# Average pooling 2x2, stride 2: the output of four loads gathered in one shared ring and stored as 63.5 KB per partition

## Chip, cores, metric

One core of one Trainium2 chip. The metric is device time in microseconds (us), the median of several executions; all runs quoted are of the fast state (the single look at one kernel has no state). The granted clock is 1.000 throughout and plays no part: nothing runs on TensorE.

## The reference

```python
# x: (32, 128, 256, 256) float32, kernel_size 2, stride 2
for i in range(h_out):
    for j in range(w_out):
        window = x[:, :, 2*i : 2*i + 2, 2*j : 2*j + 2]
        output[:, :, i, j] = np.mean(window, axis=(2, 3))
# output: (32, 128, 128, 128) float32
```

1073.7 MB are read and 268.4 MB written, each byte once. A *unit* below is one output row per partition: two input rows (2 KB) in, 512 bytes out, for each of 128 partitions. There are 4096 units.

## The kernel before

```python
sbuf = ctx.enter_context(tc.tile_pool(name="sbuf", bufs=2))
# plan: 126 parts of 32 units, then parts of 16, 8, 8 and 8, 8, 8, 4, 2, 1, 1
for parts in plan:
    in_tile = sbuf.tile([P, 32, 512], f32, name="in_tile")        # 64 KB per partition, two of them
    for g in parts:
        nc.sync.dma_start(out=it, in_=xt)                         # load queue: 64 KB per partition
        nc.vector.tensor_add(out=it[:, :, 0:w], in0=it[:, :, 0:w], in1=it[:, :, w : 2 * w])
        col_sum = sbuf.tile([P, 32, 128], f32, name="col_sum", bufs=3)
        nc.vector.tensor_add(out=col_sum[:, :g], in0=it[:, :, 0:w:2], in1=it[:, :, 1:w:2])
        nc.scalar.mul(out=col_sum[:, :g], in_=col_sum[:, :g], mul=0.25)
        nc.scalar.dma_start(out=ot, in_=col_sum[:, :g])           # store queue: 16 KB per partition
# (cut: index arithmetic, the generic path, the launch)
```

An input buffer is free again after the second add. A load is one packet of 64 KB per partition, eight per DMA engine (16 engines, 128 partitions); a store is one packet of 16 KB per partition, eight per engine.

## Time and profile before

| | before |
|---|---|
| time | 3106.51 us (3106.36 to 3106.79, 4 runs) |
| VectorE / ScalarE / DMA engines busy | 54% / 15% / all of the span |
| bytes over the span | 432 GB/s |
| one steady period (32 units) | 24.17 us |

The prediction shows the lines for these. One more view, the list of DMA issues, whose last column is the median time from issue to landing:

```profile
out_dram<-col_sum ACTq DMA_DIRECT2D x126, 2048.0 KB, 31.6
...
in_tile<-in_x_dram SPq DMA_DIRECT2D x126, 35.1
```

A 2 MB store is worth 4.8 us at 434 GB/s, yet lands 31.6 us after issue. An estimate of why: it waits about 7 us (31.6 - 24.2) for the store before it, then its eight packets per engine take turns with eight load packets: 8 x (0.61 + 2.42) = 24.2 us.

### The profile page before, as it was taken

The page shows a single profiled execution, that of the slowest core. Times are in us where ns is not written, and L with a number is a line of the kernel's source. Part 1 is how long each engine was busy: PE and PEld are TensorE (multiplying, and loading weights), DVE is VectorE, ACT ScalarE, POOL GpSimd, SP SyncE. Part 2 cuts the span into 40 slices and gives each one's busy share as a digit, 9 for nine tenths or more (in the row PEclk, how much of TensorE's full clock was granted, in tenths as well). Part 3 has the DMA queues.
Part 4 walks back from the last instruction along what each step waited for, and adds up shares of the span by engine and source line. Part 5 has one row for each costly group of instructions (what it writes and reads, how often), then busy time and mean ns, then how long its engine had stood idle before and what let it go on. Part 6 is the DMA issues. An engine that isn't in the chain of part 4 may idle for free. (4 is left out here: it accounts for less than half of the span.)

```text
span 3104.8 us, 1126 instructions
## 1 busy us (share of the span) xinstructions
DVE 1681.4 (54%) x272; ACT 465.8 (15%) x137; POOL 0.2 (0%) x4
## 2 busy tenths in 40 slices
DVE  4555555555555555555555555555555555555556
ACT  1111111111111111111111111111111111111112
POOL 0000000000000000000000000000000000000000
DMA  9999999999999999999999999999999999999999
GB/s 418 436 439 425 436 439 425 436 438 429 433 439 430 431 439 434 427 439 435 426 438 436 427 437 436 428 436 437 427 436 437 428 436 437 429 435 437 432 431 396
DMA packets 39176, 1342.26 MB, mean 432 GB/s; under 512 B 4352, under 2 KB 4736, under 8 KB 5888
## 3 DMA queue, kind: packets, MB, share of 16 engines
q1 hardware_dynamic: 19584, 1073.75, 79.8%
q10 hardware_dynamic: 19584, 268.44, 20.2%
q14 instruction: 8, 0.07, 0.0%
HBM read 1073.74 MB, written 268.44 MB: 432 GB/s over the span
## 5 line engine op out<-in xcount | busy, mean ns | idle before, releaser
L87 DVE TENSOR_TENSOR in_tile<-in_tile 128x8192 f32<-128x8192 f32 (+4 forms) x136 | 1113.9, 8190 | 1406.7 <-DMA in_tile<-in_x_dram 1406.7
L108 ACT ACTIVATE col_sum<-col_sum 128x4096 f32<-128x4096 f32 (+4 forms) x136 | 464.5, 3415 | 2635.9 <-DVE col_sum L96 2635.9
L96 DVE TENSOR_TENSOR col_sum<-in_tile 128x4096 f32<-128x4096 f32 (+4 forms) x136 | 567.8, 4175 | 13.9 <-DMA out_dram<-col_sum 1.8
L108 ACT ACT_TABLE_LOAD x1 | 1.3, 1283 | 0.7 <-PEq L190 0.7
L190 POOL MEMSET const-bfloat16-1.0<- 128x1 bf16 x1 | 0.1, 102 | 0.0
L190 POOL MEMSET const-uint8-127<- 128x1 uint8 x1 | 0.1, 102 | 0.0
L190 POOL MEMSET const-float32-0.0<- 128x1 f32 x1 | 0.1, 99 | 0.2 <-issue 0.2
L190 POOL MEMSET const-float32-1.0<- 128x1 f32 x1 | 0.1, 99 | 0.0
## 6 DMA issues: line engine op xcount, KB each, us to landing
out_dram<-col_sum ACTq DMA_DIRECT2D x126, 2048.0 KB, 31.6
in_tile<-in_x_dram SPq DMA_DIRECT2D x5, 2048.0 KB, 27.5
in_tile<-in_x_dram SPq DMA_DIRECT2D x1, 4096.0 KB, 25.5
out_dram<-col_sum ACTq DMA_DIRECT2D x5, 512.0 KB, 12.0
in_tile<-in_x_dram SPq DMA_DIRECT2D x126, 35.1
out_dram<-col_sum ACTq DMA_DIRECT2D x1, 1024.0 KB, 12.7
in_tile<-in_x_dram SPq DMA_DIRECT2D x1, 1024.0 KB, 16.2
in_tile<-in_x_dram SPq DMA_DIRECT2D x1, 512.0 KB, 16.9
```

The source lines that it names most:

```text
L87: nc.vector.tensor_add(out=it[:, :, 0:w], in0=it[:, :, 0:w], in1=it[:, :, di * w : (di + 1) * w],)
L96: nc.vector.tensor_add(out=col_sum[:, :g], in0=it[:, :, 0:wu:s], in1=it[:, :, 1 : wu + 1 : s],)
L108: nc.scalar.mul(out=col_sum[:, :g], in_=col_sum[:, :g], mul=inv)
L190: nc = _bacc.Bacc("TRN2", target_bir_lowering=False, num_devices=1)
```

## The change

The intent: fewer, longer stores and a better end. Output of four loads (31 + 32 + 32 + 32 = 127 units) collects in one buffer and leaves as one store of 63.5 KB per partition. The buffer is a ring of 158 units: groups lie alternately at units 0 to 126 and 31 to 157, so that the first piece of a group goes to the 31 units which the store under way does not read. The last group's store is issued on the load queue, behind the last loads, so that it covers the last pieces' arithmetic.

```diff
-    sbuf = ctx.enter_context(tc.tile_pool(name="sbuf", bufs=2))
-            col_sum = sbuf.tile([P, G_MAIN, w_out], mybir.dt.float32, name="col_sum", bufs=3)
-            nc.scalar.dma_start(out=ot, in_=col_sum[:, :g])
+IN_UNITS = 32
+GROUP = 127
+FIRST = GROUP - 3 * IN_UNITS
+    in_pool = ctx.enter_context(tc.tile_pool(name="inp", bufs=2))
+    out_pool = ctx.enter_context(tc.tile_pool(name="outp", bufs=1))
+    res = out_pool.tile([P, GROUP + FIRST, w_out], f32, name="res")
+    def pool(it, dst):
+        nc.vector.tensor_add(out=it[:, :, 0:w], in0=it[:, :, 0:w], in1=it[:, :, w:])
+        nc.vector.tensor_add(out=dst, in0=it[:, :, 0:w:2], in1=it[:, :, 1:w:2])
+        nc.scalar.mul(out=dst, in_=dst, mul=0.25)
+    for k in range(groups):                                       # 32 groups
+        base = 0 if k % 2 == 0 else FIRST
+        # pieces: the 31 units outside the store under way first, then 3 x 32
+        for a, g in pieces:
+            t = load(xt[:, a : a + g], g)
+            pool(t[:, :g], res[:, base + a : base + a + g])
+        if k < groups - 1:
+            nc.scalar.dma_start(out=ot, in_=res[:, base : base + GROUP])
+        else:
+            last = (ot, res[:, base : base + GROUP])
+    # rest of 32 units: loads of 16, 8, 8; then
+        if rest == 0:
+            nc.sync.dma_start(out=last[0], in_=last[1])
 (cut: index arithmetic, the pooling and storing of the rest, the old plan)
```

More of the change, by code (lines that the diff above doesn't have):

```diff
@@ L27 @@
     R = n * c * h_out
-    if k == s and 2 <= k <= 4 and R > 0 and R % P == 0:
-        _nonoverlap_pool(ctx, tc, x, out, k, n, c, h, w, h_out, w_out)
+    units = R // P if R % P == 0 else 0
+    if k == 2 and s == 2 and h % 2 == 0 and w == 256 and units >= 1024:
+        _pool_2x2(ctx, tc, x, out, units)
     else:
         _generic_pool(ctx, tc, x, out, k, s, n, c, h, w, h_out, w_out)
-def _nonoverlap_pool(ctx, tc, x, out, k, n, c, h, w, h_out, w_out):
+IN_UNITS = 32
+GROUP = 127
+FIRST = GROUP - 3 * IN_UNITS
@@ L36, in _nonoverlap_pool, with _pool_2x2 @@
+def _pool_2x2(ctx, tc, x, out, units):
     nc = tc.nc
     P = nc.NUM_PARTITIONS
-    s = k
-    R = n * c * h_out
-    hv = h_out * s
-    xs = x if hv == h else x[:, :, 0:hv, :]
-    xv = xs.rearrange("n c (ho a) w -> (n c ho) (a w)", a=s)
-    ov = out.rearrange("n c ho wo -> (n c ho) wo")
-    assert xv.shape == (R, s * w) and ov.shape == (R, w_out)
-    wu = w_out * s
-    unit_bytes = s * w * 4
-    G_MAIN = max(1, min(R // P, (64 * 1024) // unit_bytes))
-    total_units = R // P
-    nmain, rem_units = divmod(total_units, G_MAIN)
@@ L54, in _nonoverlap_pool @@
-    plan: list[list[int]] = [[G_MAIN] for _ in range(nmain)]
-    if rem_units:
-        plan.append([rem_units])
-    if G_MAIN % 32 == 0 and nmain >= 4 and rem_units == 0:
-        u = G_MAIN // 32
-        tail = [
-            [16 * u, 8 * u, 8 * u],
-            [8 * u, 8 * u, 8 * u, 4 * u, 2 * u, u, u],
-        ]
-        assert all(sum(t) == G_MAIN for t in tail)
-        plan = plan[:-2] + tail
-    sbuf = ctx.enter_context(tc.tile_pool(name="sbuf", bufs=2))
-    inv = 1.0 / float(k * k)
@@ L71, in _nonoverlap_pool @@
-    r0 = 0
-    for parts in plan:
-        in_tile = sbuf.tile([P, G_MAIN, s * w], mybir.dt.float32, name="in_tile")
-        g0 = 0
-        for g in parts:
-            rows = P * g
-            xt = xv[r0 : r0 + rows].rearrange("(p g) f -> p g f", p=P)
-            ot = ov[r0 : r0 + rows].rearrange("(p g) f -> p g f", p=P)
-            r0 += rows
-            it = in_tile[:, g0 : g0 + g]
-            g0 += g
-            nc.sync.dma_start(out=it, in_=xt)
-            for di in range(1, k):
-                nc.vector.tensor_add(
-                    out=it[:, :, 0:w],
-                    in0=it[:, :, 0:w],
-                    in1=it[:, :, di * w : (di + 1) * w],
-                )
-            col_sum = sbuf.tile(
-                [P, G_MAIN, w_out], mybir.dt.float32, name="col_sum", bufs=3
-            )
-            nc.vector.tensor_add(
-                out=col_sum[:, :g],
-                in0=it[:, :, 0:wu:s],
-                in1=it[:, :, 1 : wu + 1 : s],
-            )
-            for dj in range(2, k):
-                nc.vector.tensor_add(
-                    out=col_sum[:, :g],
-                    in0=col_sum[:, :g],
-                    in1=it[:, :, dj : wu + dj : s],
-                )
-            nc.scalar.mul(out=col_sum[:, :g], in_=col_sum[:, :g], mul=inv)
-            nc.scalar.dma_start(out=ot, in_=col_sum[:, :g])
-        assert g0 <= G_MAIN
@@ L113, in _nonoverlap_pool, with load @@
-    assert r0 == R, (r0, R)
+    f32 = mybir.dt.float32
+    w = x.shape[3]
+    w_out = w // 2
+    xv = x.rearrange("n c (ho a) w -> (n c ho) (a w)", a=2)
+    ov = out.rearrange("n c ho wo -> (n c ho) wo")
+    in_pool = ctx.enter_context(tc.tile_pool(name="inp", bufs=2))
+    out_pool = ctx.enter_context(tc.tile_pool(name="outp", bufs=1))
+    res = out_pool.tile([P, GROUP + FIRST, w_out], f32, name="res")
+    def load(src, g):
+        t = in_pool.tile([P, IN_UNITS, 2 * w], f32, name="in_tile")
+        nc.sync.dma_start(out=t[:, :g], in_=src)
+        return t
@@ new lines, in pool @@
+    def pool(it, dst):
+        nc.vector.tensor_add(out=it[:, :, 0:w], in0=it[:, :, 0:w], in1=it[:, :, w:])
+        nc.vector.tensor_add(out=dst, in0=it[:, :, 0:w:2], in1=it[:, :, 1:w:2])
+        nc.scalar.mul(out=dst, in_=dst, mul=0.25)
+    groups, rest = divmod(units, GROUP)
+    if rest == 0:
+        groups, rest = groups - 1, GROUP
+    last = None
+    for k in range(groups):
+        r0 = k * GROUP * P
+        xt = xv[r0 : r0 + GROUP * P].rearrange("(p g) f -> p g f", p=P)
+        ot = ov[r0 : r0 + GROUP * P].rearrange("(p g) f -> p g f", p=P)
+        base = 0 if k % 2 == 0 else FIRST
+        spans = [(FIRST + i * IN_UNITS, IN_UNITS) for i in range(3)]
+        if base == 0:
+            pieces = [(0, FIRST)] + spans
+        else:
+            pieces = [(3 * IN_UNITS, FIRST)] + [(a - FIRST, g) for a, g in spans]
+        for a, g in pieces:
[3 more added lines that the diff above has]
+            nc.scalar.dma_start(out=ot, in_=res[:, base : base + GROUP])
+        else:
+            last = (ot, res[:, base : base + GROUP])
@@ new lines, in _pool_2x2 @@
+    r0 = groups * GROUP * P
+    while rest:
+        n = min(rest, IN_UNITS)
+        t = in_pool.tile([P, IN_UNITS, 2 * w], f32, name="in_tile")
+        tout = in_pool.tile([P, IN_UNITS, 2 * w], f32, name="in_tile")
+        to = tout[:].rearrange("p g f -> p (g f)").rearrange("p (g f) -> p g f", f=w_out)
+        cuts = [n // 2, n // 4, n - n // 2 - n // 4] if n >= 8 else [n]
+        a, parts = 0, []
+        for g in cuts:
+            xt = xv[r0 : r0 + g * P].rearrange("(p g) f -> p g f", p=P)
+            ot = ov[r0 : r0 + g * P].rearrange("(p g) f -> p g f", p=P)
+            nc.sync.dma_start(out=t[:, a : a + g], in_=xt)
+            parts.append((ot, a, g))
+            a += g
+            r0 += g * P
+        rest -= n
+        if rest == 0:
+            nc.sync.dma_start(out=last[0], in_=last[1])
+        for ot, a, g in parts:
+            pool(t[:, a : a + g], to[:, a : a + g])
+            nc.scalar.dma_start(out=ot, in_=to[:, a : a + g])
```

## The prediction

> **What bounds the kernel now.** I read the page first, its busy shares and its row of DMA slices.
>
> ```profile
> DVE 1681.4 (54%) x272; ACT 465.8 (15%) x137; POOL 0.2 (0%) x4
> ...
> DMA  9999999999999999999999999999999999999999
> ...
> q1 hardware_dynamic: 19584, 1073.75, 79.8%
> q10 hardware_dynamic: 19584, 268.44, 20.2%
> ```
>
> VectorE works 54% of the span and ScalarE 15%, while the DMA engines stand at 9 in all forty slices: the load queue takes 79.8% of their time and the store queue 20.2%, together all of it. The bytes are fixed by the task: 1073.75 MB in, 268.44 MB out, 1342.2 MB. Second, the waits, to see who starves:
>
> ```profile
> ACT col_sum L108 <- DVE col_sum L96: 2635.9, 136, 33.9
> DVE in_tile L87 <- DMA in_tile<-in_x_dram: 1406.7, 133, 22.7
> DVE col_sum L96 <- DMA out_dram<-col_sum: 1.8, 3, 0.9
> ```
>
> VectorE waits for loads in 133 of 136 pieces; a wait for a store to free an output buffer exists three times, 1.8 us in all, at the very end. Third, the timeline of one steady stretch:
>
> ```profile
> 1494.01 8.69 DVE L87 TENSOR_TENSOR in_tile<-in_tile 128x8192 f32<-128x8192 f32 x1 [10.97 <-DMA in_tile<-in_x_dram]
> 1502.79 4.42 DVE L96 TENSOR_TENSOR col_sum<-in_tile 128x4096 f32<-128x4096 f32 x1
> ...
> 1507.25 3.62 ACT L108 ACTIVATE col_sum<-col_sum 128x4096 f32<-128x4096 f32 x1 [20.56 <-DVE col_sum L96]
> 1510.89 0.34 ACTq L110 DMA_DIRECT2D out_dram<-col_sum  x1
> 1518.19 8.69 DVE L87 TENSOR_TENSOR in_tile<-in_tile 128x8192 f32<-128x8192 f32 x1 [10.97 <-DMA in_tile<-in_x_dram]
> ```
>
> One period is 1518.19 - 1494.01 = 24.18 us (others 24.16); VectorE needs 8.69 + 4.43 = 13.1 us of it. A period moves 8.39 MB in and 2.10 MB out, so 10.49 MB in 24.17 us = 434 GB/s. Fourth, the same by stretches, to find where the rate is not 434:
>
> ```profile
> 2500.00:3000.00 500.00, 267.44 (x41) 75.47 (x21) 0.00 (x0) 1.00 1.00 433
> ...
> 3050.00:3060.00 10.00, 8.57 (x3) 3.48 (x1) 0.00 (x0) 1.00 0.98 419
> 3060.00:3070.00 10.00, 7.97 (x4) 3.10 (x3) 0.00 (x0) 1.00 1.01 434
> 3070.00:3080.00 10.00, 4.36 (x3) 1.06 (x1) 0.00 (x0) 1.00 1.01 431
> 3080.00:3090.00 10.00, 6.20 (x4) 1.87 (x2) 0.00 (x0) 1.00 0.99 419
> 3090.00:3100.00 10.00, 7.23 (x8) 2.33 (x4) 0.00 (x0) 1.00 0.82 332
> 3100.00:3104.80 4.80, 0.58 (x2) 0.63 (x3) 0.00 (x0) 1.00 0.33 111
> ```
>
> The last two columns are DMA share and GB/s. Only the last 15 us fall off. Against 434, the missing bytes of these six stretches are worth 0.35 + 0 + 0.07 + 0.35 + 2.35 + 3.57 = 6.7 us. That, the start, and the last fraction of a per cent between 434 and the ceiling are all a change of this kind can win.
>
> **What the Trainium skill says.** (1) "DMA: Bandwidth & Descriptors", section "Where 436 GB/s comes from": 16 ports give 435.2 GB/s. The trace agrees: 434 in the steady part and, in the first stretch without a store, 8.39 MB between the first add at 22.70 and the next at 42.02, so 19.32 us or 434 too. Loads alone and loads mixed with stores run at the same rate. (2) Same page, "Why small descriptors are slow (HBM only)": a fixed overhead of about 3 cycles per packet. The trace has something of that size: at 27.2 GB/s per engine, one engine's 8 x 65,536 + 8 x 16,384 bytes of a period take 24.094 us; measured 24.17, so 0.076 us over 18 packets (8 data and one semaphore packet in each of two queues): 4.2 ns a packet. (3) Same page, "Queues, rings and completion order": an engine goes round-robin between its queues, a packet of typically 9 to 17 descriptors at a time. The single-packet records of this trace show the turns but finer: around 1506 to 1512 us 32 load packets of 64 KB and 32 store packets of 16 KB start in 6.05 us, two of each per engine (2.42 + 0.61 us a pair), so one descriptor each in turn. (4) "SBUF — State Buffer", section "SBUF size: 192, 224, or 256?": about 208 KiB per partition are usable. The change takes 2 x 64 + 158 x 0.5 = 207 KiB; it fits barely, and no run yet shows it.
>
> **The change, part by part.**
> *Arithmetic.* The same adds and multiply on the same elements, in pieces of 31 or 32 units. VectorE stays near 1681 us, off the path: worth 0.
> *Fewer packets.* Before: 136 loads and 136 stores, 9 packets per engine each, 272 x 9 = 2448. After: 4096 units are 32 groups of 127 and a rest of 32, so 32 x 4 + 3 = 131 loads and 32 + 3 = 35 stores, 166 x 9 = 1494. The 954 packets fewer, at 4.2 ns, give 4.0 us. (The packet records would say more: 611 ns for 16 KB and 2418 for 64 KB fit 9.7 ns plus 36.7 ns per 1000 bytes, and 954 times 9.7 ns would be 9 us. But the durations overlap: summed over an engine they give 3107 us where the data lasted 3102. I take the 4.2 from the period.)
> *Bytes.* 1342.2 MB at 435.2 GB/s: 3084.1 us, before and after.
> *Tail.* Before, loads shrink to 256 KB, each followed by add, add, multiply and a store, so the DMA runs dry for 6 to 7 us. After, the last group's 8.3 MB store is issued behind the last three loads. Counting from the landing of the last full piece: its adds and multiply end at +16.7 us, when the store is issued; the last loads (8.39 MB, 19.3 us) still have about 2.6 us to go, so there is no gap. VectorE does the rest, 4.43 + 2.29 and twice 2.29 + 1.23 us, from +13.1 to about +27; the last small store is issued by +28. The DMA still has the 19.2 us big store plus 4.8 us of small ones, and is busy to about +43. It never runs dry; what remains is the last completion and the engines' uneven finish, estimated at 2.8 us (loads alone land 22.70 - 19.32 - 1.7 = about 1.7 us after their bytes would be through).
> *Sum.* Before: 3084.1 + 2448 x 0.0042 = 10.3, start 1.7 (first data packet), three hiccups in the 24.17 us rhythm 2.6, leaves 3104.8 - 3098.7 = 6.1 for the tail, near the 6.7 above. After: 3084.1 + 6.3 + 1.7 + 2.6 + 2.8 = 3097.5 us of span. The time before is 3106.64 - 3104.8 = 1.8 above its span: 3099.3, a gain of 7 us or 0.24%.
>
> **The rivals.**
> *A ring wait opens holes.* Pieces two to four of a group overwrite what the previous group's store reads, while the first goes to the 31 free units. Take the store's issue as zero. The load of piece one has 19.3 - 16.7 = 2.6 us left and piece two's was issued 3.6 us earlier. With turns of one descriptor the store needs 8 x (2.40 + 2.42) = 38.5 us, landing near +40. Piece two needs all its 8 packets and the 1.1 left of piece one: +41 or later, its first add ends near +51, and only its second add writes the ring. Margin about 10 us: no wait. And a wait that did occur would cost only if both input buffers filled and the store ended, when neither queue has work. If the store got one turn in two, it would land near +60 after about both loads, leaving some 5 us empty per group, 31 x 5 = 155 us: 3255. The observed one-to-one turns speak against it.
> *The ring is guarded as a whole.* If every write into the shared buffer waited for the store, piece one too would wait, both input buffers would fill, and after each store about 4.4 us of add and 2 us of load latency would be empty: 31 x 6.4 = 200 us, 3300. Against it: in the tail of the kernel before several loads write parts of one input buffer while VectorE works on others, at 419 to 434 GB/s.
> *The new layout changes the rate.* Partitions now lie 254 KB apart for loads and 63.5 KB for stores, instead of 64 and 16. If long stores ran 1% slower than bytes say, that is 6 us: 3105. The rate has been the same with and without stores so far, which is for no change.
> *The tail gain is swallowed.* If the large last store straggles on single engines by several of its 2.4 us packets, 3 to 5 us come back: 3103.
>
> **Range and chances.** No route leads to 2% faster: with no overhead at all 3084.1 + 1.8 is 0.7% below. The centre is 3099. The full packet saving of the records would give about 3094, a straggling tail or slightly slower stores 3103 to 3106. I take 3093 to 3107, 94% for within 2%, 5% for one of the two ring waits, 1% for faster.
>
> **What would show it.** Right: DMA at 9 in all slices and 434 to 435 GB/s; first-add intervals near 19.3 us without a store in flight and up to 39 us with one; stores landing 39 to 43 us after issue; hardly any VectorE wait for a store; about 430 GB/s until 3 us before the end; 131 x 144 = 18,864 load and 5,040 store packets. Wrong: VectorE's second add waiting on the store some 31 times with DMA slices under 9 (a ring wait), a steady rate under 430 (layout), or more than 5 us of falling rate at the end (tail).

## The result, and the profile after

The changed kernel takes **3304.39 us** (3298.40 to 3324.51, 4 runs) against 3106.51: slower, ratio 1.0649, 95% interval 1.0618 to 1.0679. (A ratio is the mean time of one kernel's runs over that of the other's of the same rounds, so not quite the ratio of the medians quoted.) The prediction was 3099 us, with 5% for slower. It was wrong.

The page of the changed kernel:

```profile
DVE 1679.8 (51%) x262; ACT 464.7 (14%) x132; POOL 0.2 (0%) x4
...
DMA  9999999999999999999999999999999999999998
GB/s 428 415 418 405 400 416 393 427 401 404 411 400 423 398 400 415 396 412 403 402 405 405 403 414 405 403 405 403 414 405 403 405 403 414 405 404 416 392 419 378
...
q1 hardware_dynamic: 19008, 1082.07, 78.4%
q10 hardware_dynamic: 4896, 260.11, 18.4%
```

VectorE's work is what it was. The row of DMA tenths still reads 9 in all slices but the last, which hides the loss, because 9 means 90% or more. The rate has fallen to about 405 GB/s, and the two queues together take 96.8% of the engines' time. The waits:

```profile
ACT res L67 <- DVE res L66: 2811.4, 128, 42.5
DVE in_tile L65 <- DMA in_tile<-in_x_dram: 1592.5, 128, 32.8
```

No wait for a store is among them: the feared ring wait did not come. VectorE waits for loads, as before, only longer. One group in the timeline:

```profile
1530.46 0.34 ACTq L87 DMA_DIRECT2D out_dram<-res  x1
1532.68 8.43 DVE L65 TENSOR_TENSOR in_tile<-in_tile 128x7936 f32<-128x7936 f32 x1 [5.91 <-DMA in_tile<-in_x_dram]
...
1577.24 8.69 DVE L65 TENSOR_TENSOR in_tile<-in_tile 128x8192 f32<-128x8192 f32 x1 [31.81 <-DMA in_tile<-in_x_dram]
1586.03 4.43 DVE L66 TENSOR_TENSOR res<-in_tile 128x4096 f32<-128x4096 f32 x1
...
1596.60 8.69 DVE L65 TENSOR_TENSOR in_tile<-in_tile 128x8192 f32<-128x8192 f32 x1 [6.15 <-DMA in_tile<-in_x_dram]
...
1635.43 8.43 DVE L65 TENSOR_TENSOR in_tile<-in_tile 128x7936 f32<-128x7936 f32 x1 [5.82 <-DMA in_tile<-in_x_dram]
```

A group lasts 1635.43 - 1532.68 = 102.75 us. The first group, which had no store beside it, took 76.8 us; with a store's 8.3 MB at 434 GB/s, 19.2 us, a group should last 96. The store and the second piece share the 44.6 us to 1577.24. The piece after it lands 19.4 us later, but in that last stretch the DMA engines stand still (columns as in the prediction's fourth view; a packet counts where it starts, so a share can exceed 1):

```profile
1574.00:1586.00 12.00, 8.69 (x1) 0.00 (x0) 0.00 (x0) 1.00 0.98 426
1586.00:1588.00 2.00, 1.97 (x1) 0.00 (x0) 0.00 (x0) 1.00 0.38 164
1588.00:1589.00 1.00, 1.00 (x1) 0.00 (x0) 0.00 (x0) 1.00 0.16 66
1589.00:1591.00 2.00, 1.45 (x1) 0.51 (x1) 0.00 (x0) 1.00 0.00 0
1591.00:1592.00 1.00, 0.00 (x0) 1.00 (x1) 0.00 (x0) 1.00 3.12 1049
```

From about 1588 to 1591.4 almost nothing moves; then all start at once. The end of the hole is VectorE's: the buffer of the second piece is free at 1586.03 + 4.43 = 1590.46, and only then is the fourth piece's load issued. The third piece's load, queued all the while, should have filled this time. The single-packet records of the trace show why it did not. Each engine writes one completion packet per load; sorted, in us:

```
second group, first piece, no store beside it yet:  97.8 ... 98.6              (16 engines within 0.8)
              second piece, beside the first store: 134.5 ... 135.7   137.1   143.6
the group shown, first piece:                       1527.4 ... 1528.2          and 1532.3
                 second piece:                      1563.6 ... 1566.9          and 1576.9
                 third piece:                       1587.7 ... 1589.1          and 1596.2
```

Fifteen engines are together and **one is behind**: 8 us after the very first store beside a load, some 10 us after each later store. Its packets are longer during the store: in the group shown seven of its eight store packets take 2.87 to 3.07 us where every other engine's take 2.40. A load has landed when the last engine has landed, so VectorE starts by the slow engine, and the fifteen have nothing left to fetch.

How far may one engine fall behind? From the slowest engine's completion it takes 0.3 us to VectorE's start (1576.9 to 1577.24), 13.2 us for both adds and 0.9 us from issue to the first packet (1590.46 to 1591.4) until the next-but-one load moves: 14.5 us. The fifteen need 19.3 us for the load between. The difference, **4.8 us, is all the slack that two buffers give**. In the group shown the engine is 8.3 us behind in the third piece (1587.9 for most, 1596.2); the others stand still for about 3 us and begin with a slow packet, and are then some 4.4 us ahead (median of all groups), close to the slack, until the next store (1527.5 and 1532.3 are the same stage of the cycle). The trace doesn't name the engines, but the end of one packet and the start of the next can be followed: in the group shown, the slow engine's sixteen packets from 1532.31 to 1576.88 leave no pause and last 44.57 us, 6.0 more than 8 x (2.42 + 2.40). Of these, 4.1 come from the seven store packets and 1.9 from two load packets. So the slow engine is never waiting, and the whole core goes at its pace.

For the experiments I add up the packet records of each kernel in two figures, both per engine (mean of 16): *idle*, the time with no packet under way over the whole span, and *slow*, the time by which packets exceed the median duration of their kind. Before: 8.4 idle, 1.4 slow. After: 112.5 idle, 97.4 slow. The slow part is mostly loads: the first packets on engines that had run dry take 2.7 to 3.6 us instead of 2.42, those at the beginning of a store 3.4 to 4.4.

### The profile page after: what moved, and what is told of

It reads as the page before. It is cut to its first block, busy times and chain, and to the rows that moved or that the text cites. A ratio compares the mean times of both kernels' runs of the same rounds, so it can differ in the third digit from the quotient of the medians.

```text
span 3300.4 us, 893 instructions
## 1 busy us (share of the span) xinstructions
DVE 1679.8 (51%) x262; ACT 464.7 (14%) x132; POOL 0.2 (0%) x4
## 3 DMA queue, kind: packets, MB, share of 16 engines
q1 hardware_dynamic: 19008, 1082.07, 78.4%
q10 hardware_dynamic: 4896, 260.11, 18.4%
## 4 chain that ended last, share of the span: by engine, by line
DMA 52%; DVE 31%; another core or an unknown queue 16%; issue 0%; DVEq 0%; ACT 0%
DMA in_tile<-in_x_dram 52%; DVE in_tile L65 21%; DVE res L66 10%; DVE in_tile L66 0%; DVEq L66 0%; ACT in_tile L67 0%
## 5 line engine op out<-in xcount | busy, mean ns | idle before, releaser
L65 DVE TENSOR_TENSOR in_tile<-in_tile 128x8192 f32<-128x8192 f32 (+2 forms) x131 | 1113.1, 8497 | 1592.5 <-DMA in_tile<-in_x_dram 1592.5
L67 ACT ACTIVATE res<-res 128x4096 f32<-128x4096 f32 (+1 forms) x128 | 459.4, 3589 | 2811.4 <-DVE res L66 2811.4
L66 DVE TENSOR_TENSOR res<-in_tile 128x4096 f32<-128x4096 f32 (+1 forms) x128 | 562.2, 4392 | 10.5
## 6 DMA issues: line engine op xcount, KB each, us to landing
out_dram<-res ACTq DMA_DIRECT2D x31, 8128.0 KB, 46.4
out_dram<-in_tile ACTq DMA_DIRECT2D x1, 1024.0 KB, 19.2
```

What stands on the lines that cost most here:

```text
L66: nc.vector.tensor_add(out=dst, in0=it[:, :, 0:w:2], in1=it[:, :, 1:w:2])
L67: nc.scalar.mul(out=dst, in_=dst, mul=0.25)
```

## The experiments

Names in the expectations: LAG is the account just given; the others are explained there. Where they give the slack as 3.6, 8 and 12.3 us they still use a landing delay of 1.7 us from the prediction; the completion packets show 0.3, which makes 4.8, 9.2 and 13.6. In each the edit is against the changed kernel. The table gives all eighteen; what each tells follows. "Slow stores" are packets of the group stores over 1.15 of their median; "spread" is from the first to the last engine's landing of a load, median and ninth decile.

| kernel | time us | idle | slow | slow stores | spread |
|---|---|---|---|---|---|
| before | 3106.5 | 8.4 | 1.4 | 0 | 2.0, 2.8 |
| changed | 3304.4 | 112.5 | 97.4 | 171 | 5.3, 13.1 |
| e1_four16 | 3104.9 | 7.5 | 1.9 | 0 | 2.8, 3.8 |
| e2_each_piece | 3105.3 | 7.1 | 2.3 | 0 | 3.0, 4.5 |
| e3_both16 | 3136.4 | 7.9 | 13.2 | 0 | 3.3, 6.3 |
| e4_load16 | 3137.8 | 7.4 | 11.5 | 36 | 2.5, 3.7 |
| e5_two32 | 3156.5 | 7.8 | 46.2 | 0 | 3.6, 5.3 |
| e6_load32 | 3168.6 | 22.1 | 44.8 | 426 | 9.1, 17.0 |
| e7_group120 | 3213.9 | 52.3 | 68.5 | 0 | 1.3, 3.3 |
| e8_stream (wrong) | 3105.8 | 7.6 | 4.4 | 0 | 4.7, 4.8 |
| e9_one_add (wrong) | 3132.0 | 9.7 | 27.8 | 100 | 10.6, 17.7 |
| e10_same_queue | 3108.8 | 6.8 | 11.7 | 0 | 2.7, 3.0 |
| e11_half_add (wrong) | 3159.3 | 20.9 | 50.3 | 160 | 9.1, 12.7 |
| e12_no_vector (wrong) | 3105.9 | 6.4 | 4.1 | 0 | 2.0, 4.4 |
| e13_scalar_slow (wrong) | 3772.8 | 524.7 | 155 | 568 | 0.9, 9.1 |
| e14_scalar_late (wrong) | 3310.6 | 152.8 | 89.2 | 90 | 14.7, 30.7 |
| e15_group124 | 3164.0 | 29.0 | 45.4 | 0 | 1.9, 4.1 |
| e16_group125 | 3127.1 | 6.4 | 26.0 | 1 | 1.9, 3.8 |
| e17_group126 | 3128.1 | 12.4 | 24.0 | 0 | 2.5, 4.5 |
| e18_same_queue126 | 3130.9 | 15.5 | 24.9 | 0 | 2.5, 3.1 |

"Wrong" marks results that are wrong on purpose. Idle, slow and spread come from each kernel's profiled execution, the time is the median of its runs (the execution profiled was the slowest of four for e14, 3335.4, and the fastest for e12, 3102.2); beside each, the kernel before took 3106.4 us. With the 66 thousand short load packets of e3 and e4, 1 ns in the median is 4 us of slow, so there the figure is rough.

### Is it the layout, the gathering, or the length of the packets?

**e1_four16**, the group's store as four of 16 KB per partition:

```diff
-            nc.scalar.dma_start(out=ot, in_=res[:, base : base + GROUP])
+            for a, g in pieces[1:] + pieces[:1]:
+                nc.scalar.dma_start(out=ot[:, a : a + g], in_=res[:, base + a : base + a + g])
```

> The group's store leaves at the same moment, but as four stores of 16 KB per partition (15.5 for one); loads and layout as changed. Theory SIZE (a 63.5 KB store packet taking turns with loads is what is slow): 3095 to 3106, intervals between first adds near 24.2 us, no stretch of 44 us, store packets at 611 ns. Theory LAYOUT (partitions 254 KB apart make mixed traffic slow): stays near 3300. Theory BURST (a store queue that empties and starts anew costs some 6.6 us per group, whatever the packet): turns of one packet let 32 small store packets last about 97 us, so the queue hardly empties and BURST also says about 3105; this run separates LAYOUT from the other two only.

**e2_each_piece**, each piece stored when it is scaled:

```diff
             pool(t[:, :g], res[:, base + a : base + a + g])
-        if k < groups - 1:
-            nc.scalar.dma_start(out=ot, in_=res[:, base : base + GROUP])
+            if k < groups - 1 or a != pieces[-1][0]:
+                nc.scalar.dma_start(out=ot[:, a : a + g], in_=res[:, base + a : base + a + g])
 (cut: the last piece's store is held back, as `last`)
```

> Layout of the changed kernel, each piece stored as soon as it is scaled, as before the change (16 KB per partition); only the last piece's store is held back behind the last loads. SIZE and BURST: 3097 to 3104, a little under the kernel before, because only the tail is new. LAYOUT: near 3300.

Measured 3104.90 (ratio to before 0.9995, 0.9980 to 1.0010) and 3105.28 (0.9997, 0.9982 to 1.0012). Ring, group, layout and moment of the store (in e1) are those of the changed kernel, so LAYOUT falls, and so does any cost of gathering as such. The list of issues of e1 reads like the one of before, 31 and 35 us:

```profile
out_dram<-res ACTq DMA_DIRECT2D x93, 2048.0 KB, 31.0
...
in_tile<-in_x_dram SPq DMA_DIRECT2D x96, 35.0
```

In the changed kernel the same two rows are:

```profile
out_dram<-res ACTq DMA_DIRECT2D x31, 8128.0 KB, 46.4
...
in_tile<-in_x_dram SPq DMA_DIRECT2D x96, 49.8
```

The difference of the two profiled spans is 3300.4 - 3103.4 = 197.0 us; idle and slow grow by 105.0 and 95.5. Together they are 200.5, so the two figures cover the loss (they are bookkeeping and name no cause).

**e3_both16**, e1 with loads cut to 16 KB packets, and **e4_load16**, the one long store with such loads:

```diff
-        nc.sync.dma_start(out=t[:, :g], in_=src)
+        for i in range(0, g, 8):
+            j = min(i + 8, g)
+            nc.sync.dma_start(out=t[:, i:j], in_=src[:, i:j])
```

> Stores as four of 16 KB at the group's end, and each load cut into four of 8 units, so that load packets are 16 KB too. With equal packets the store again lasts about 38 us and its queue then stands empty for some 57 us: a burst with small packets. SIZE: 3100 to 3115 (more packets cost about 4 us). BURST: near 3300, since the queue restarts 31 times. LAYOUT: near 3300.

> Store as one of 63.5 KB per partition as in the changed kernel; loads cut to 16 KB packets. Turns of one packet give the store 80% of an engine, so it should land about 24 to 26 us after issue instead of 46. If SIZE is about the store packet alone, the start (2.7 us a group) and the slow engine stay: about 3250 to 3300. If it is about two long packets alternating: under 3150. BURST: near 3300.

Measured 3136.42 and 3137.79. Here the store queue empties 31 times with small packets (e3) or with a long store and short loads (e4), and neither idles. So BURST is small: in e3 some 11 us more of slow packets than in e1; the other 20 us over e1 go with four times as many load packets (65.9 thousand against 16.8 thousand; not separated further). e4 lands its store 27.9 us after issue, because with turns of one packet a long store packet outweighs a short load packet four to one:

```profile
out_dram<-res ACTq DMA_DIRECT2D x31, 8128.0 KB, 27.9
```

Both lengths matter: a long store is nearly harmless beside short loads, long loads beside short stores.

**e5_two32**, the group's store as two of about 32 KB, and **e6_load32**, four input buffers of 16 units:

```diff
 (e5)
-            nc.scalar.dma_start(out=ot, in_=res[:, base : base + GROUP])
+            cut = 64 if base else 63
+            for a, g in ((0, cut), (cut, GROUP - cut)):
+                nc.scalar.dma_start(out=ot[:, a : a + g], in_=res[:, base + a : base + a + g])
 (e6)
-IN_UNITS = 32
+IN_UNITS = 16          # bufs=4; first pieces of 15 and 16, then six of 16; ring as before
```

> As the changed kernel, but the group's store leaves as two stores of 31.5 to 32 KB per partition; loads keep 64 KB packets. The theory now (PAIR: a long load packet alternating with a long store packet is what is slow; 16 KB on either side removed most of it) expects something between: start of the mixed stretch about half of 2.7 us a group, slow stores fewer, idle engines under 1 us a group: 3130 to 3200. If the loss has a threshold near 64 KB: 3100 to 3110. If any gathered store beside 64 KB loads is slow: near 3300.

> Store of 63.5 KB as changed, loads of 16 units (32 KB packets) in four buffers of half the size, same bytes of buffer. PAIR: between the 3137 of 16 KB loads and 3304: 3140 to 3230. If the idle engines come from having only two buffers (rival HOLE: pieces of the next load cannot be issued until the slowest engine has landed the one before), four buffers remove about 3.4 us x 31 = 104 us whatever the packet: 3190 to 3210, with packets as slow as in the changed kernel.

Measured 3156.47 and 3168.56: between, as PAIR had it, with neither a threshold at 64 KB nor the 3190 to 3210 that HOLE gave for e6. In e6 many engines have slow store packets (426) and differ by 9 us and more, but with four buffers they idle 22 us instead of 112, as HOLE had it; the packets became quicker as well (slow 45 instead of 97).

### Is it the turns alone?

**e8_stream**, no arithmetic, stores that wait for nothing (ScalarE's queue took them one after another, the last of them at about 989 us):

```diff
-            pool(t[:, :g], res[:, base + a : base + a + g])
+    nc.vector.memset(res[:], 0.0)        # once; no pooling anywhere
 (cut: the stores of the rest read the ring too)
```

> Wrong results on purpose: no arithmetic. Loads as changed, only waiting for a buffer's earlier load; stores of a zeroed ring, all issued at once, so 63.5 KB stores and 64 KB loads alternate for the first 1235 us or so, started once, then loads alone. If one engine is slow at each long store next to a long load (PAIR), the mixed part runs at about 5.4 instead of 4.82 us per pair on that engine and the whole at its pace: mixed part near 1385 us, idle engines there some 10%, total about 3230. If the loss is only in starting the mixture: one start, total 3095 to 3105.

Measured 3105.82 (one look). The theory's own number, 3230, was wrong. With the store queue always full, long packets alternate at full rate; the stretches with a store beside every load look like the one without:

```profile
200.00:400.00 200.00, 0.00 (x0) 0.00 (x0) 1.00 1.00 434
...
2000.00:3000.00 1000.00, 0.00 (x0) 0.00 (x0) 1.00 1.00 434
```

So long packets in turn are not slow of themselves. What e8 lacks is the new start of a store in every group, and loads that wait for arithmetic.

**e10_same_queue**, the same packets in one queue, the store behind the next group's second load:

```diff
+            if i == 1 and held is not None:
+                nc.sync.dma_start(out=held[0], in_=held[1])
-            nc.scalar.dma_start(out=ot, in_=res[:, base : base + GROUP])
+            held = (ot, res[:, base : base + GROUP])
```

> Correct kernel. The same 63.5 KB stores and 64 KB loads, the same ring and pieces, but each group's store is issued on the load queue, behind the second load of the next group, so that the two kinds of packet follow each other in one queue instead of taking turns. LAG (taking turns makes one engine's packets 3.0 us instead of 2.4; it falls 8.7 us behind per store, and with two buffers the other fifteen run dry and start anew): no slow packets, no idle engines, 3096 to 3103, so faster than the kernel before by 4 to 10 us. Rival LONG STORE (a long store beside loads is slow wherever it is queued, or gathering as such costs): above 3150. Rival RING (the second piece must wait for the store, which now ends some 42 us after it is ready): VectorE waits for the store 31 times, but the third load is behind the store in the queue, so no gap and the same 3096 to 3103; if there is a gap, about 3200.

Measured 3108.81 (3106.16 to 3112.00, ratio 1.0007, 0.9993 to 1.0021): the loss is gone, LONG STORE falls, though the promised gain over before did not come; 11.7 us of slow packets remain. It also shows a harmless ring wait:

```profile
DVE res L66 <- DMA out_dram<-res: 329.3, 31, 11.3
```

VectorE waits for the store in 31 groups, 329 us in all, and idle stays at 6.8 us: the load queue holds work behind the store. A wait is only worth what the bound engine loses by it.

### Is it the slack?

**e9_one_add** leaves the first add out, **e11_half_add** does it for half of each piece:

```diff
 (e9)
-        nc.vector.tensor_add(out=it[:, :, 0:w], in0=it[:, :, 0:w], in1=it[:, :, w:])
 (e11)
+        h = it.shape[1] // 2
+        nc.vector.tensor_add(out=it[:, :h, 0:w], in0=it[:, :h, 0:w], in1=it[:, :h, w:])
```

> Wrong results on purpose: the first of the two adds is left out, so VectorE frees an input buffer 4.4 instead of 13.1 us after landing. HOLE: the 104 us in which engines stand idle go, about 3200. If the slow engine sets the pace and the others only wait for it: unchanged, 3290 to 3310.

> Wrong results on purpose: the first add covers half of each piece, so an input buffer is free about 8.8 us after landing (13.1 as changed: 3304 us; 4.4 with one add: 3132). LAG: the fifteen engines may be 3.6 us ahead as changed, 12.3 with one add, 8 here; a lag of 8.7 to 13 us per store no longer empties them for long: 3140 to 3220, idle engines 20 to 60 us in all instead of 104. If only the packets' own slowness mattered and not the slack: 3290 to 3310.

With the buffer free 13.1, 8.8 and 4.4 us after VectorE's start (slack 4.8, 9.2 and 13.6 us) the times are 3304, 3159 (3142 to 3184) and 3132, idle 112, 21 and 10. e11 came in as LAG had it; e9 came out far under both its expectations, because slow packets fell as well, 97 to 28 us. The engines are no closer together (spread 9.1 and 10.6 us), and yet hardly idle: with more slack, unequal engines make no hole. That is shown.

It is not the whole of the gain. By LAG alone one engine that loses 6 us at each of 31 stores would have used up even 13.6 us within three groups (an estimate from the group shown), and the core would again go at its pace. The records show that the lone straggler is gone too. From the fifteenth engine's landing of a load to the last engine's is 4.4 us in the changed kernel (median; 10.1 for the piece beside the store), 0.7 in e11 and 0.6 in e9. In the changed kernel each of the 31 stores has 4 to 7 slow packets; in e9 and e11 most stores have none, others up to 20 and 38, which is several engines, as each has only eight. So slack and straggler went together, and these runs don't say which led: the two edits also shorten VectorE's work and move the store's issue forward, with the buffer's release.

**e7_group120** fits the arithmetic of the slack, by accident. With groups of 120 the first piece has 24 units and lasts 14.5 us, no more than the 14.5 needed:

```diff
-GROUP = 127
+GROUP = 120
```

> Correct kernel, groups of 120 units: stores of 60 KB per partition at a pitch of 60 KB, loads at a pitch of 240 KB (multiples of 4 KB instead of 512 B and 2 KB). If the odd pitch of 63.5 KB is what makes one engine slow: 3096 to 3110. LAG, with packets nearly as long: 34 groups instead of 32, so 3290 to 3330.

Measured 3213.91, neither number. No store packet was slow and the engines stayed together (spread 1.3), yet 35.9 us of the run between its start and its end are idle, 1.06 us in each of 34 groups: with no slack at all, small differences between engines suffice, and slow first packets follow each time (68.5 us). I had not seen that the short first piece would do this; the run therefore says little on pitch or length.

### What sets one engine back?

**e12_no_vector** has ScalarE copy a quarter of each piece into the ring; **e13_scalar_slow** spends as long on the input buffer as the adds did; **e14_scalar_late** frees the buffer early and issues the store late:

```diff
-        nc.vector.tensor_add(...)    # both adds and the multiply
+ (e12)  nc.scalar.mul(out=dst, in_=it[:, :, 0 : w // 2], mul=0.25)
+ (e13)  mul over it[:, :, 0:w]; mul over it[:, :, 0:80]; mul it -> dst; mul dst -> dst
+ (e14)  mul it -> dst; then four muls within dst (128, 128, 128, 64 wide)
```

> Wrong results on purpose: VectorE does nothing in the 32 groups, ScalarE copies a quarter of each input piece into the ring and frees the buffer 3.6 us after landing. If VectorE's traffic made the packets slow (rival VECTOR): no slow store packets at all, 3096 to 3106. LAG: slow packets remain as with one add (some 100 stores over 2.76 us), but no idle engines: 3120 to 3140.

> Wrong results on purpose: VectorE idle, ScalarE holds each input buffer for about 12.9 us (a pass over half of the piece, a small one, a copy into the ring) and issues the store some 16.5 us after landing, so the timing of the changed kernel without VectorE. LAG and SLACK (what matters is that the next-but-one load is issued 13 us after landing and the store close to the border between two loads): slow store packets on one engine and idle engines return, 3280 to 3310. VECTOR (VectorE's traffic sets off the slow packets): as with the fast ScalarE version, 3100 to 3120.

> Wrong results on purpose: as the fast ScalarE version (buffer free 3.6 us after landing, 3106 us, no slow store), but ScalarE works on in the ring so that the store is issued about 16.5 us after landing, near the border between two loads, as in the changed kernel. If the moment of the store sets off the slow packets: some 100 or more slow stores, no idle engines thanks to the slack, 3120 to 3140. If the short queue of loads (slack) sets them off: 3100 to 3117, no slow stores.

e12 measured 3105.94 (3102.20 to 3117.26) with no slow store, where LAG had expected 100 of them. That spoke for VECTOR, but e13 and e14, with VectorE idle, have 568 and 90 slow stores: VectorE is not needed. For the one straggler this rests on e14; in e13 up to 35 packets of a store are slow, so several engines are. The trace of the changed kernel says the same: in the first group with a store the slow engine's packets at 112.9, 118.8, 130.0 and 135.4 us are long while VectorE has nothing to do from 111.8 to 143.98.

Both e13 and e14 went astray otherwise, and neither met a number expected of it. In e13 the passes of two pieces were interleaved on ScalarE, so the first piece's buffer was released only after the second had landed, and 525 us of idling followed:

```profile
1519.42 2.27 ACT L66 ACTIVATE in_tile<-in_tile 128x2480 f32<-128x2480 f32 x1
1558.82 7.03 ACT L65 ACTIVATE in_tile<-in_tile 128x8192 f32<-128x8192 f32 x1 [37.13 <-DMA in_tile<-in_x_dram]
1565.76 3.49 ACT L67 ACTIVATE res<-in_tile 128x3968 f32<-128x3968 f32 x1
```

In e14 the copy itself writes the ring and waits for the store, which keeps the buffer:

```profile
1594.53 3.62 ACT L65 ACTIVATE res<-in_tile 128x4096 f32<-128x4096 f32 x1 [34.52 <-DMA out_dram<-res]
```

What e14 against e12 still shows is that with a store issued late, close to the border between two loads, one engine falls 13 to 33 us behind while fifteen stay within 1.7 us (median), and with the store issued 13 us earlier (3.6 instead of 16.5 us after ScalarE's start) none does. Whether the moment or the buffer held longer does it, e14 cannot say.

**e15_group124**, **e16_group125**, **e17_group126**, **e18_same_queue126** vary the length of the store and the pitch of partitions:

```diff
-GROUP = 127
+GROUP = 124    # e15: rest of 4 units
+GROUP = 125    # e16: 64 further units pooled and stored at 16 KB before the first group
+GROUP = 126    # e17: 32 such units; e18: the same in e10's form
```

> Correct kernel, groups of 124: stores of 62 KB per partition at a pitch of 62 KB, loads at 248 KB; the first piece of 28 units lasts 16.9 us, a little more than the 15.8 from landing to the first packet of the next-but-one load, which with 24 units (14.5 us) it did not. If the pitch of 63.5 KB, not a multiple of 1 or 2 KB, makes the one engine slow: no store packet over 1.15 of the median and 3150 to 3220 (cold starts remain). If it is length or chance: a lagging engine as with 127, 3270 to 3310.

> Correct kernel, groups of 125: stores of 62.5 KB per partition at a pitch of 62.5 KB, an odd multiple of 512 bytes as with 127 (63.5), but shorter than the 62 KB + 2% of 127; first piece 29 units (17.5 us). The 64 units more that are left over are loaded, pooled and stored at 16 KB before the first group, so that the end is as with 127. If an odd multiple of 512 bytes sets one engine back (PITCH): 100 or more slow stores, lag of one engine, 3250 to 3310. If it is only the length near 64 KB (LENGTH): like 124 without its idle end, 3135 to 3155, no slow store.

> Correct kernel, groups of 126: 63 KB at a pitch that is an odd multiple of 1 KB; first piece 30 units; 32 units before the first group. PITCH: no or few slow stores, 3125 to 3160. LENGTH: between 124 and 127, 3180 to 3300, slow stores.

> Correct kernel, groups of 126 with each store on the load queue behind the second load of the next group (3108.8 with 127). If the 10 us of slow loads left there come from the 63.5 KB pitch: 3096 to 3102, the fastest correct kernel. If they come from the change between the kinds of packet: 3104 to 3112.

Measured 3164.04, 3127.11, 3128.13 and 3130.90. e15 and e17 lie within the numbers of the pitch theory, e16 under both of its numbers. In none does one engine lag. 125 has an odd multiple of 512 bytes as pitch, like 127, so PITCH in that form falls; 126 differs from 127 by 0.8% in length, so a steady growth with LENGTH falls. In e15 about 20 us are its idle end (the rest of 4 units covers nothing). e16 and e17 keep about 25 us of slow packets, 0.8 us a group, at the starts. In e17 the stretch with the store is 37 us instead of 44.6:

```profile
1567.08 8.16 DVE L65 TENSOR_TENSOR in_tile<-in_tile 128x7680 f32<-128x7680 f32 x1 [4.92 <-DMA in_tile<-in_x_dram]
...
1604.06 8.69 DVE L65 TENSOR_TENSOR in_tile<-in_tile 128x8192 f32<-128x8192 f32 x1 [24.62 <-DMA in_tile<-in_x_dram]
```

e18 did not become the fastest kernel; against e10 it has more slow loads (24 against 10 us), which I cannot explain. No correct kernel is clearly faster than the one before: e1 and e2 are at 0.9995 and 0.9997 with 1 inside the interval.

**What stays open:** why exactly one engine runs its store packets at 3.0 us with groups of 127 and none with 120, 124, 125 or 126 (the last two also begin with small stores, which I did not vary alone). With 127 it appears when the store starts late beside loads short of work and not in e8 or e12. A rival stands untested: the experiments ran on chips 1, 11, 12 and 14, the record names no chip for the changed kernel, and it was not run again beside them, so 127 against 125 and 126 may also be chip against chip. Against this speaks that on chip 14 e14, with 127, has the straggler and e15, with 124, has not; but the two differ in more than the length.

## Why the prediction was wrong

*Its bound was right.* The kernel lives by its DMA engines; VectorE's busy time (1679.8 us), the packet counts (19,008 load queue, 4,896 store queue: 18,864 and 5,040 with the last store moved to the load queue) and the 207 KB of buffers came as said.

*The step that failed* is the working under "A ring wait opens holes": the store needs 38.5 us in turns, lands near +40, piece two lands at +41, and from that "no wait". Measured: the store landed 46.4 us after issue (median), and piece two let VectorE start at +46.8 in the group shown. The group took 102.75 us instead of 96, and over 31 stores the loss came to 198 us, for which the sum had no term. The "no wait" for the ring itself held. The working stood on two assumptions. First, that the sixteen engines advance as one; one of them fell 5 to 13 us behind, which no view of the kernel before shows, where the landings of a load lie within 2.0 us (median). Second, that a hole needs a wait for the store. The prediction had the right picture, both buffers full and neither queue with work, and tied it to one cause. I computed VectorE's margin at the ring (10 us, and it held), but not the slack of the load queue, 19.3 - 14.5 = 4.8 us, though nearly every term stood in the profile. That was the narrow one.

*"The rate has been the same with and without stores"* was taken from 16 KB packets in a store queue that never emptied, and carried over to 63.5 KB packets that start anew each group. e1 and e8 show how narrow the ground was: with either the short packets or the never empty queue the rate is indeed kept; with neither it fell to 419 GB/s in the mixed stretch and 394 in the rest of the group (windows 1532.68 to 1577.24 and on to 1635.43). The rival "new layout" guarded against 1% of store time; the layout was innocent (e2), the size was 6%.

*The packet saving of 4.0 us* was not measured by itself. e12 has the changed kernel's packets without the loss: its lowest run, 3102.2, lies 3 us under e2's 3105.3, which would fit, but its median, 3105.9, shows no saving. (The larger figure in brackets is also a little off: a line through 611 and 2418 ns has 8.7 ns and 36.8 ns per 1000 bytes, so 8 us and not 9. Nothing rests on it.)

*The landing delay of 1.7 us* was wrong too: 22.70 - 19.32 - 1.7 also holds the slow first packets (2.7 to 3.4 us instead of 2.42); from completion to VectorE it is 0.3 to 0.4 us.

*The tail* failed in its size: 2.8 us of loss were estimated; the last 40 us of the changed kernel idle 6.4 us per engine against 6.3 before, because its engines finish apart and the lag makes a gap at 3270 to 3275. In e1 and e2, without lag, it is 5.5 and 5.1: a gain of one us, not three.

*The signs named* for being wrong: the VectorE wait on the store with slices under 9 did not appear. A steady rate under 430 did (407 GB/s from 100 to 3200 us), but it was to stand for the layout, which e1 and e2 clear. First-add intervals of 44.6 instead of up to 39 us, and stores landing after 46.4 instead of 39 to 43, broke the list of what would be right, and pointed nearer to the cause.

## What to carry to other kernels

In a kernel bound by its DMA engines, work out the slack of the load queue before lengthening anything: time of one load minus (landing delay + compute until the buffer is free + issue delay). Here it was 4.8 us, and an engine that fell further behind held up the whole core. Longer packets save little once they are 16 KB (an estimated 4 us of 3106 here) and make each turn, each start and each straggler coarser; where a long store is wanted, the same queue as the loads or a free buffer earlier took most or all of the loss away (e10 3108.8, e9 3132.0 us).

## What the Trainium skill lacked or had wrong

- "DMA: Bandwidth & Descriptors", section "Queues, rings and completion order", has engines change queues after packets of 9 to 17 descriptors typically. Here they change after every record of 64 KB, which the prediction takes for one descriptor (the trace doesn't say how many a record holds): two loads and two stores per engine in 6.05 us before; and the long store lands after 27.9 us beside 16 KB loads, after 46.4 beside 64 KB loads.
- The same page, "Rules for kernel authors", advises to coalesce many small transfers into one large, with no upper bound. In this kernel stores of 16 KB per partition (2 MB) gave 3104.9 us, the same bytes at 63.5 KB (8.3 MB) 3304.4, and 3108.8 where they shared the loads' queue.
- The same page notes, for another kind of contention ("iDMA fabric"), that a bulk load runs at the pace of its slowest engine; no page says that plain loads and stores issued as here can set one engine back (a row on two engines being usually slower, in "Latency and other measured facts", guesses at another way of issuing): landings of one load within 2.0 us (median) before, one engine up to 13 us behind after, with store packets of 3.0 instead of 2.40 us; nor that a pair of input buffers bears only the slack worked out above.
- The pages have the latency of a first byte, but none says that the first packets themselves last longer: on idle engines a 64 KB load packet takes 2.7 to 3.4 us instead of 2.42 (first packets of the kernel before), and 3.4 to 4.4 when a store starts with it.
- "SBUF — State Buffer", section "SBUF size: 192, 224, or 256?": about 208 KiB usable is right as far as tried; 207 KiB built, ran and gave correct results.
